# Row maximum of a streamed tensor: other load sizes, and a last row without halves

## The chip, the cores and the metric

The kernel runs on one core of a Trainium2 chip. The metric is the device time of one execution in microseconds (us). Executions of the kernel before took 166.0 to 166.5 us.

Names used below: DVE is VectorE, which does the reductions. SP is SyncE, whose queue issues the loads. ACT is ScalarE, whose queue issues the two stores. A load is cut into packets, one for each of 128 partitions, and 16 DMA engines move 8 of these packets each. A load has *landed* when its semaphore has been stepped by all 16 of them.

## The reference

```python
batch, seq, dim = 32, 512, 1024
x = np.random.randn(batch, seq, dim).astype(np.float32)   # 67.1 MB

def reference(x):
    return np.max(x, axis=-1).astype(np.float32)          # 16384 maxima
```

The 16,384 rows are dealt out to 128 partitions, 128 rows each. Below, "a row" is one row on every partition at once: 128 x 1024 elements, 512 KB.

## The kernel before

It streams the input into a ring of 46 rows in SBUF. Each load brings some rows to all partitions, and one reduction on DVE follows each load. Load sizes fall towards the end, so that little is left to reduce when the last byte has come. The last row is loaded and reduced in two halves, and a maximum combines them.

```python
ROWS = [10, 13, 12, 10, 9, 8, 7, 7, 6, 5, 5, 4, 4, 3, 3, 3, 3, 2, 2, 2, 2, 2, 1, 1, 1, 1, 1]
RING = 46
...
    for g in ROWS:
        if at + g > RING:
            at = 0
        xc = ring[:, at:at + g, :]
        nc.sync.dma_start(out=xc, in_=xr[:, b:b + g, :])
        nc.vector.reduce_max(out=res[:, b:b + g], in_=xc, axis=X)
        at += g
        b += g
        if not stored and b >= I - 16:      # I = 128: the results of 112 rows go out early
            stored = b
            nc.scalar.dma_start(out=out_r[:, :b], in_=res[:, :b])

    assert b == I - 1 and at + 1 <= RING
    for h in range(2):                      # the last row, in halves
        xh = ring[:, at, h * H:(h + 1) * H]
        nc.sync.dma_start(out=xh, in_=xr[:, b, h * H:(h + 1) * H])
        nc.vector.reduce_max(out=part[:, h:h + 1], in_=xh, axis=X)
    nc.vector.tensor_tensor(out=res[:, b:b + 1], in0=part[:, 0:1], in1=part[:, 1:2],
                            op=mybir.AluOpType.max)
    nc.scalar.dma_start(out=out_r[:, stored:], in_=res[:, stored:])
```

A load into a part of the ring that still holds unreduced rows waits until they are reduced. The trace shows a second limit: the loads and stores share eight semaphores, so a ninth DMA waits for the first to land.

Of the kernel before, what the change touches and what calls it, by code (L numbers as in the profile page):

```python
# [1 line left out]

# [4 lines left out]


F32 = mybir.dt.float32


ROWS = [10, 13, 12, 10, 9, 8, 7, 7, 6, 5, 5, 4, 4, 3, 3, 3, 3, 2, 2, 2, 2, 2, 1, 1, 1, 1, 1]
RING = 46


@with_exitstack
def kernel(
    ctx: ExitStack,
    tc: tile.TileContext,
    x: bass.AP,  # L20
    out: bass.AP,
):
    nc = tc.nc
    P = 128
    X = mybir.AxisListType.X

    xf = x.flatten_outer_dims()
    N, D = xf.shape
    H = D // 2
    I = N // P  # L30

    xr = xf.rearrange("(p i) d -> p i d", p=P)
    of = out.flatten_outer_dims()
    out_r = bass.AP(tensor=of.tensor, offset=of.offset, ap=[[I, P], [1, I]])

    once = ctx.enter_context(tc.tile_pool(name="once", bufs=1))
    ring = once.tile([P, RING, D], F32)
    res = once.tile([P, I], F32)
    part = once.tile([P, 2], F32)

    b = at = 0
    stored = 0
# [8 lines that stand above are left out]
        if not stored and b >= I - 16:  # L51
            stored = b
            nc.scalar.dma_start(out=out_r[:, :b], in_=res[:, :b])

    assert b == I - 1 and at + 1 <= RING
    for h in range(2):
        xh = ring[:, at, h * H:(h + 1) * H]
        nc.sync.dma_start(out=xh, in_=xr[:, b, h * H:(h + 1) * H])
        nc.vector.reduce_max(out=part[:, h:h + 1], in_=xh, axis=X)  # L59
    nc.vector.tensor_tensor(  # L60
        out=res[:, b:b + 1], in0=part[:, 0:1], in1=part[:, 1:2],
        op=mybir.AluOpType.max,
    )
    nc.scalar.dma_start(out=out_r[:, stored:], in_=res[:, stored:])


# [1 line left out]
_INS = ['x']  # L68
_OUTS = [((32, 512), 'float32')]


# [23 lines left out]
```

## Time and profile before

| what | value | where it is read |
|---|---|---|
| time, median of four runs | 166.22 us | the runs |
| span of the profiled run | 164.7 us | the page |
| first load (10 rows) lands | 15.80 us | semaphore records |
| last load (half a row) lands | 160.74 us | semaphore records |
| DVE's last instruction ends | 162.40 us | timeline |
| the last store lands | 163.85 us | semaphore records |

The page of the kernel before: the span and DVE's busy time (busy, share of the span, instructions); the span in 40 slices, with busy tenths of DVE and of the DMA engines; the chain of waits by line; and the groups of DVE's instructions (busy us, mean ns of one | idle before them, and what ended it).

```profile
span 164.7 us, 118 instructions
DVE 139.5 (85%) x30; POOL 0.2 (0%) x4
...
DVE  0001994399989999999999989999999999999994
...
DMA  6998999999989999999999999999999999999960
...
DMA ring<-in_x_dram 70%; DVE res L48 27%; DVE part L59 1%; DVE res L60 0%
...
L48 DVE TENSOR_REDUCE res<-ring 128x2 f32<-128x2048 f32 (+11 forms) x27 | 138.1, 5165 | 22.9 <-DMA ring<-in_x_dram 22.7
L59 DVE TENSOR_REDUCE part<-ring 128x1 f32<-128x512 f32 x2 | 1.3, 676 | 0.0
L60 DVE TENSOR_TENSOR res<-part 128x1 f32<-128x1 f32 x1 | 0.2, 159 | 0.0
```

The slices decide: the DMA engines are busy from the second slice to the 38th, whereas DVE idles for much of the first eight and catches up. DVE's 85% is large only because the two rates are close. The groups kept apart by shape give DVE's rate:

```profile
L48 DVE TENSOR_REDUCE res<-ring 128x10 f32<-128x10240 f32 x2 | 21.6, 10816 | 15.8 <-DMA ring<-in_x_dram 15.8
...
L48 DVE TENSOR_REDUCE res<-ring 128x13 f32<-128x13312 f32 x1 | 14.0, 14020 | 4.9 <-DMA ring<-in_x_dram 4.9
...
L48 DVE TENSOR_REDUCE res<-ring 128x1 f32<-128x1024 f32 x5 | 5.7, 1208 | 0.0
```

Three more rows cost 14.020 - 10.816 = 3.204 us, that is 1.068 us a row, plus 0.14 us an instruction. Five single rows are busy for only 5.7 us with overlaps counted once, not 6.0: the next one starts 0.08 us before the one in front has ended, so one starts every 1.13 us. The loads bring a row every 1.23 us on average, a single row every 1.28 us.

Last, the timeline of the end of the kernel before (start us, us, engine, line, operation, count; "q" marks the issue of a DMA):

```profile
158.69 2.33 DVE L48 TENSOR_REDUCE res<-ring 128x1 f32<-128x1024 f32 x2
160.94 1.27 DVE L59 TENSOR_REDUCE part<-ring 128x1 f32<-128x512 f32 x2
162.25 0.16 DVE L60 TENSOR_TENSOR res<-part 128x1 f32<-128x1 f32 x1
162.44 0.34 ACTq L64 DMA_DIRECT2D out_dram<-res  x1
```

The last half has landed at 160.74 us, when DVE has not yet begun even the first half. 1.66 us pass from that landing to the end of the maximum.

### The profile page before, as it was taken

Reading aid. Unit: us, or ns where it says so; the run is one execution under the profiler, and the core shown is the slowest. Engines: PE = TensorE matmul, PEld = TensorE weight load, DVE = VectorE, ACT = ScalarE, POOL = GpSimd, SP = SyncE. Lnnn points to the kernel's source line nnn. Section 1 sums busy time; section 2 is a strip of 40 time slices with the busy share of each in tenths; the row PEclk is TensorE's granted clock in tenths of the full one; section 3 lists DMA queues with packets and bytes.
Section 4 is the critical chain, followed back from the end, with each engine's and each line's share of the span. In section 5 each row is a group of like instructions: output and inputs, shape, how many; then the busy total and the mean of one; then the engine's idle time right before and its main releaser. Section 6 shows DMA issues by size and latency. Waiting matters only on the chain.

```text
span 164.7 us, 118 instructions
## 1 busy us (share of the span) xinstructions
DVE 139.5 (85%) x30; POOL 0.2 (0%) x4
## 2 busy tenths in 40 slices
DVE  0001994399989999999999989999999999999994
POOL 0000000000000000000000000000000000000000
DMA  6998999999989999999999999999999999999960
GB/s 199 438 467 376 453 465 453 436 406 394 469 388 467 444 430 430 408 438 425 439 432 425 426 431 419 428 438 409 438 430 421 427 421 421 420 418 421 408 260 2
DMA packets 4464, 67.18 MB, mean 408 GB/s; under 512 B 752, under 2 KB 752, under 8 KB 1648
## 3 DMA queue, kind: packets, MB, share of 16 engines
q1 hardware_dynamic: 4176, 67.11, 95.8%
q10 hardware_dynamic: 288, 0.07, 0.2%
HBM read 67.11 MB, written 0.07 MB: 408 GB/s over the span
## 4 chain that ended last, share of the span: by engine, by line
DMA 70%; DVE 28%; issue 0%
DMA ring<-in_x_dram 70%; DVE res L48 27%; DVE part L59 1%; DVE res L60 0%
## 5 line engine op out<-in xcount | busy, mean ns | idle before, releaser
L48 DVE TENSOR_REDUCE res<-ring 128x2 f32<-128x2048 f32 (+11 forms) x27 | 138.1, 5165 | 22.9 <-DMA ring<-in_x_dram 22.7
L59 DVE TENSOR_REDUCE part<-ring 128x1 f32<-128x512 f32 x2 | 1.3, 676 | 0.0
L60 DVE TENSOR_TENSOR res<-part 128x1 f32<-128x1 f32 x1 | 0.2, 159 | 0.0
L79 POOL MEMSET const-bfloat16-1.0<- 128x1 bf16 x1 | 0.1, 101 | 0.0
L79 POOL MEMSET const-uint8-127<- 128x1 uint8 x1 | 0.1, 101 | 0.0
L79 POOL MEMSET const-float32-0.0<- 128x1 f32 x1 | 0.1, 98 | 0.2 <-issue 0.2
L79 POOL MEMSET const-float32-1.0<- 128x1 f32 x1 | 0.1, 98 | 0.0
## 6 DMA issues: line engine op xcount, KB each, us to landing
ring<-in_x_dram SPq DMA_DIRECT2D x2, 5120.0 KB, 35.6
ring<-in_x_dram SPq DMA_DIRECT2D x2, 3584.0 KB, 33.0
ring<-in_x_dram SPq DMA_DIRECT2D x1, 6656.0 KB, 30.4
ring<-in_x_dram SPq DMA_DIRECT2D x1, 6144.0 KB, 44.4
ring<-in_x_dram SPq DMA_DIRECT2D x4, 1536.0 KB, 38.9
ring<-in_x_dram SPq DMA_DIRECT2D x2, 2560.0 KB, 38.1
ring<-in_x_dram SPq DMA_DIRECT2D x5, 1024.0 KB, 22.2
ring<-in_x_dram SPq DMA_DIRECT2D x1, 4608.0 KB, 43.1
```

The costliest lines, as they stand in the source:

```text
L48: nc.vector.reduce_max(out=res[:, b:b + g], in_=xc, axis=X)
L59: nc.vector.reduce_max(out=part[:, h:h + 1], in_=xh, axis=X)
L60: nc.vector.tensor_tensor(out=res[:, b:b + 1], in0=part[:, 0:1], in1=part[:, 1:2], op=mybir.AluOpType.max,)
L79: nc = _bacc.Bacc("TRN2", target_bir_lowering=False, num_devices=1)
```

## The change

The intent: the sizes start at 14 and fall without a rise, there are eight single rows at the end in place of five, and the last row comes whole, so that there is no second reduction and no combining maximum behind it.

```diff
-ROWS = [10, 13, 12, 10, 9, 8, 7, 7, 6, 5, 5, 4, 4, 3, 3, 3, 3, 2, 2, 2, 2, 2, 1, 1, 1, 1, 1]
+ROWS = [14, 14, 11, 11, 9, 8, 8, 7, 6, 5, 5, 4, 4, 3, 3, 2, 2, 2, 2, 1, 1, 1, 1, 1, 1, 1, 1]
...
-    assert b == I - 1 and at + 1 <= RING
-    for h in range(2):
-        xh = ring[:, at, h * H:(h + 1) * H]
-        nc.sync.dma_start(out=xh, in_=xr[:, b, h * H:(h + 1) * H])
-        nc.vector.reduce_max(out=part[:, h:h + 1], in_=xh, axis=X)
-    nc.vector.tensor_tensor(
-        out=res[:, b:b + 1], in0=part[:, 0:1], in1=part[:, 1:2],
-        op=mybir.AluOpType.max,
-    )
+    assert b == I
     nc.scalar.dma_start(out=out_r[:, stored:], in_=res[:, stored:])
```

Both lists reach row 112 at the end of a load: the old one after 17 loads, the new one after 15. The first 112 rows are the *head*, the last 16 the *tail*.

More of the change, by code (lines that the diff above doesn't have):

```diff
@@ L28 @@
     N, D = xf.shape
-    H = D // 2
     I = N // P
@@ L38 @@
     res = once.tile([P, I], F32)
-    part = once.tile([P, 2], F32)
     b = at = 0
```

## The prediction

> **What bounds the kernel now.** The stream of loads. The page's busy line says VectorE (DVE) 85%, but its slices show the DMA engines near 0.9 from the second slice to the 38th. From the landing of the first load (10 rows, 15.80 us) to that of the last two-row load (122 rows in all, 153.08 us) a row takes 1.226 us, 428 GB/s; by the groups by form, reductions take 1.068 us a row plus 0.14 us an instruction (13 rows 14.02 us, one row 1.21 us). DVE is faster than the loads and runs behind only by what one load brings at once. The Trainium skill, "VectorE: DVE Perf Modes", perf-mode tier table, gives tensor_reduce only the 1x mode; 1024 elements at its 0.96 GHz are 1.067 us, as this trace has it. "DMA: Bandwidth & Descriptors", Specifications, gives a fabric ceiling of 435 GB/s; at 428, no load pattern can gain much there. The chain of waits credits DVE with 28%, but most of that is backlog absorbed by the next landing.
>
> **What counts** is: the start, 128 rows of stream, and what follows the last landing. Before: the last half row lands at 160.74, DVE still has 0.8 us of backlog and starts it at 161.54, ends 162.21; the maximum ends at 162.40; the store is issued at 162.44, lands at 163.85; end 164.7.
>
> **What the change does.**
> - First load 14 rows: DVE starts near 20.6 instead of 15.8 us. Off the critical path: it catches up at 0.137 us a row.
> - Only three loads (39 of 46 rows) fit before the ring wraps, where four did. The fourth waits for the first reduction (ends about 35.7 us), but the queue holds work until about 50. I stepped through the ring, the limit of eight DMAs in flight and both rates: the smallest margin in mid-run is about 9 us. The first store still leaves at row 112, near 144 us, and lands near 150.6; a single-row load that reuses its semaphore waits for it, with about 1.8 us of queued work left. Tight, but enough.
> - DMA overhead: about 0.075 us a load (one row 1.28 us, three rows 3.69 us). 27 loads for 29; but the halves landed 0.62 to 0.63 us apart, so the gain is 0.05 to 0.15 us.
> - Tail: eight singles land every 1.28 us and DVE takes 1.12 us from start to start, so the backlog of about 0.8 us shrinks by 0.16 each and is gone before the last. The last reduction starts as its row lands and takes 1.21 us. Before, landing to end of the maximum was 1.66 us. Gain 0.45 us, less any residue.
>
> **Sum.** -0.1 (loads) -0.4 (tail) = -0.5 us of 166.26: 165.8 us; range 165.2 to 166.5. Faster by over 2%: 1%; within 2%: 98%; slower: 1%.
>
> **What would show it.** The last load lands at 160.5 to 160.8; one reduction of 1.21 us stands behind it and no maximum; DVE idles 20.6 us at first; DMA slices stay at 9; no gap of the load stream near 152 us.
>
> **What would make it wrong.** (1) One DMA engine fell 0.67 us behind the other fifteen at 65.9 us (a 36,864-byte packet took 2.15 us instead of 1.36) and every later load ended on it. If that is chance, the difference can be anything between 0 and -1.1 us. (2) The single-row load that waits for the store leaves the queue empty: up to 1 us lost. (3) Backlog left at the last row: up to 0.5 us lost.

(The 1.067 us a row that it works out from the page's clock is an estimate; the trace's own figure is the 1.068 us.)

## The result, and the profile after

The changed kernel took 165.62 us (median of four runs, 165.41 to 165.81) against 166.22 us (166.00 to 166.53). The ratio is 0.9962, with a 95% interval of 0.9942 to 0.9982. Here and below a ratio is the mean time of one kernel's fast runs over that of the other's fast runs of the same rounds, so it is not quite the ratio of the medians that are quoted. The forecast was 165.8 us and "within 2%".

The same lines of the page after:

```profile
span 163.8 us, 111 instructions
DVE 138.7 (85%) x27; POOL 0.2 (0%) x4
...
DVE  0000099978999999999999999999999999999993
...
DMA  6999999989999989999999999999999999999980
...
DVE res L46 57%; DMA ring<-in_x_dram 41%; SPq L45 0%
...
L46 DVE TENSOR_REDUCE res<-ring 128x1 f32<-128x1024 f32 (+10 forms) x27 | 138.7, 5202 | 22.7 <-DMA ring<-in_x_dram 22.6
```

DVE starts at 20.75 us in place of 15.82 and idles 22.7 us in all, against 22.9 us before: the late start is made up while the DMA slices stay full. A trap in this page is the chain of waits. DVE's share doubles, from 28% to 57%, though DVE does less work and the loads still set the pace. The last piece of that chain, in order of time, is:

```profile
94.69 66.64 DVE res L46 x21
```

After the reduction that starts at 94.69 us DVE has no gap: each one starts just before the one in front has ended, 0.02 to 1.01 us after its own row landed, so the chain never steps over to a load. Only the last of these lags counts.

The end of the changed kernel, from the timeline:

```profile
157.81 3.52 DVE L46 TENSOR_REDUCE res<-ring 128x1 f32<-128x1024 f32 x3
161.37 0.34 ACTq L54 DMA_DIRECT2D out_dram<-res  x1
```

The table sets the landings of the last pieces, from the semaphore records, beside the starts of their reductions, from the instruction records. The lag is the difference.

| before: piece | lands | starts | lag | after: piece | lands | starts | lag |
|---|---|---|---|---|---|---|---|
| | | | | single 1 | 151.18 | 152.18 | 1.00 |
| single 1 | 154.36 | 155.31 | 0.95 | single 3 | 153.74 | 154.43 | 0.69 |
| single 3 | 156.92 | 157.56 | 0.64 | single 5 | 156.30 | 156.68 | 0.38 |
| single 5 | 159.49 | 159.82 | 0.33 | single 7 | 158.86 | 158.94 | 0.08 |
| first half | 160.12 | 160.94 | 0.82 | single 8 | 160.09 | 160.11 | 0.02 |
| second half | 160.74 | 161.54 | 0.80 | | | | |

The single rows wear the backlog down by 0.155 us each, in both kernels. Before, the halves build it up again: the first half lands 0.63 us after a single row that takes DVE 1.2 us.

Between the two profiled runs the difference is 164.73 - 163.82 = 0.91 us. That is more than the 0.60 us between the medians: the profiled run of before, at 166.5 us, stands at the slow end of its four. It splits into three parts:

| part | before | after | difference |
|---|---|---|---|
| start to the last landing | 160.74 | 160.09 | -0.65 |
| last landing to DVE's last end | 1.66 | 1.24 | -0.42 |
| DVE's last end to the end of the span | 2.33 | 2.49 | +0.16 |

The second line is the tail that was predicted. The other two raised questions.

**The first line.** The prediction had seen that one DMA engine fell 0.67 us behind in the profile of before. The steps of the last load's semaphore put a number on it: fifteen engines were done at 160.10 us before and at 160.07 us after, and the sixteenth at 160.74 and at 160.09. So by the undisturbed engines the stream was shorter by only 0.03 us. But was the delay chance, or did the old sizes invite it?

**The third line** turned out to be SP's closing sequence. After its last load SP waits for the eight DMA semaphores in pairs, in a fixed order, with four instructions about 0.07 us apart. Here are SP's waits for the output in the view of waits (us in total, times, longest), first before, then after:

```profile
SPq L90 <- DMA out_dram<-res: 3.1, 1, 3.1
```

```profile
SPq L80 <- DMA out_dram<-res: 11.4, 1, 11.4
```

With 29 loads and two stores, the last store used a semaphore of the third pair; the first two pairs had been passed before it landed. With 27 loads it uses one of the first pair: SP stops there for 11.4 us, and has three more waits to walk through afterwards. From the landing of the store to the end of the span it is 0.88 us before and 1.01 us after; the rest of the 0.16 us is the store itself, 1.42 us from issue to landing before and 1.45 after.

### The profile page after: what moved, and what is told of

It reads as the page before. It is cut to its first block, busy times and chain, and to the rows that moved or that the text cites. A ratio compares the mean times of both kernels' runs of the same rounds, so it can differ in the third digit from the quotient of the medians.

```text
span 163.8 us, 111 instructions
## 1 busy us (share of the span) xinstructions
DVE 138.7 (85%) x27; POOL 0.2 (0%) x4
## 4 chain that ended last, share of the span: by engine, by line
DVE 57%; DMA 41%; SPq 0%; issue 0%
DVE res L46 57%; DMA ring<-in_x_dram 41%; SPq L45 0%
## 5 line engine op out<-in xcount | busy, mean ns | idle before, releaser
L46 DVE TENSOR_REDUCE res<-ring 128x1 f32<-128x1024 f32 (+10 forms) x27 | 138.7, 5202 | 22.7 <-DMA ring<-in_x_dram 22.6
```

## The experiments

Theory A: what lasts of the gain is behind the last landing; the heads differ only by two loads, and the rest of the first line is one engine's chance delay. Rival B: the new sizes make the stream itself shorter, or spare it such delays.

Twelve runs were made, in three calls of four, each call on one chip, which are named P, Q and R in order. Chip and time of a call are not parted by this: "chip Q" below means the chip at the time of that call. (The chip of the first comparison is not known.) All results were correct. The kernel before ran beside each call: 166.94 us on P (166.1 to 167.81), 167.00 on Q (166.35 to 167.32), 165.93 on R (165.87 to 166.26). No two calls can be compared by raw times.

### New head alone (chip P)

The kernel before, old tail with halves and maximum, with the head of the changed one:

```diff
-ROWS = [10, 13, 12, 10, 9, 8, 7, 7, 6, 5, 5, 4, 4, 3, 3, 3, 3, 2, 2, 2, 2, 2, 1, 1, 1, 1, 1]
+ROWS = [14, 14, 11, 11, 9, 8, 8, 7, 6, 5, 5, 4, 4, 3, 3, 2, 2, 2, 2, 2, 1, 1, 1, 1, 1]
```

> Only the load sizes of the first 112 rows are the new ones; the last 16 rows, the halves and the maximum are as before. Theory A (all of the lasting gain is in what follows the last landing, and the 0.65 us by which the last load landed earlier in the profile is one DMA engine's chance delay): the time is that of before within 0.15 us (ratio 0.999 to 1.001), landing of the last load to end of the maximum stays 1.66 us. Rival B (the new sizes of the large loads make the stream shorter, or keep an engine from falling behind): 0.3 to 0.65 us faster (ratio 0.996 to 0.998), last load landing near 160.1.

Measured: 166.16 us (165.85 to 166.50, six runs), ratio 0.9958 (0.9930 to 0.9986). From last landing (160.51) to the end of the maximum it is 1.66 us again:

```profile
160.71 1.27 DVE L59 TENSOR_REDUCE part<-ring 128x1 f32<-128x512 f32 x2
162.01 0.16 DVE L60 TENSOR_TENSOR res<-part 128x1 f32<-128x1 f32 x1
```

The tail behaves as theory A says, but the time does not. Theory A expected no gain and the interval excludes that: on this chip the new head was worth something by itself. This went for rival B, though not in every point: B had the last load land near 160.1 us, and in this profile, which has late DMA packets (below), it landed at 160.51.

### New tail alone (chip P)

```diff
-ROWS = [10, 13, 12, 10, 9, 8, 7, 7, 6, 5, 5, 4, 4, 3, 3, 3, 3, 2, 2, 2, 2, 2, 1, 1, 1, 1, 1]
+ROWS = [10, 13, 12, 10, 9, 8, 7, 7, 6, 5, 5, 4, 4, 3, 3, 3, 3, 2, 2, 2, 2, 1, 1, 1, 1, 1, 1, 1, 1]
(and no halves, no maximum, as in the changed kernel)
```

> Only the last 16 rows are the new ones (four loads of two rows, eight of one, no halves, no maximum); the first 112 rows are as before. Theory A: 0.4 us faster than before (ratio 0.997 to 0.998), last landing to end of the last reduction 1.21 to 1.25 us. Rival B: within 0.15 us of before, because the stream is what got shorter.

Measured: 166.43 us (165.44 to 166.95), ratio 0.9968 (0.9934 to 1.0002). The last row lands at 160.10 us and its reduction, below, ends 1.24 us later.

```profile
160.13 1.22 DVE L46 TENSOR_REDUCE res<-ring 128x1 f32<-128x1024 f32 x1
```

The profile is what theory A expected (1.21 to 1.25 us). The ratio agrees with it too but is not clear of 1; the clean measure came later, on chip R.

### Before, with a whole last row (chip P)

```diff
-ROWS = [10, 13, ..., 2, 1, 1, 1, 1, 1]
+ROWS = [10, 13, ..., 2, 1, 1, 1, 1, 1, 1]
(and no halves, no maximum, as in the changed kernel)
```

It parts the tail's gain into the halves' going and the longer row of singles.

> Before, with its last row loaded and reduced whole: no halves and no maximum, six single rows at the end where the changed kernel has eight. Theory A: DVE still starts the last row about 0.17 us after it landed (the backlog shrinks by 0.155 us a single), so last landing to end is about 1.38 us and the gain 0.25 us (ratio 0.998 to 0.999): more than half of the tail's gain is the halves' going, the rest the longer row of singles. If the halves' going were all, it would be 0.42; if it were nothing, 0. Rival B: no gain.

Measured: 166.73 us (166.01 to 167.37), ratio 0.9982 (0.9946 to 1.0019): not clear of 1. The profile is clearer. The last row lands at 161.15 us, and the reduction starts 0.27 us later and ends 1.48 us after the landing:

```profile
161.42 1.21 DVE L46 TENSOR_REDUCE res<-ring 128x1 f32<-128x1024 f32 x1
```

The expectation was a lag of 0.17 us. The last two rows had landed only 1.24 and 1.22 us apart, not 1.28, so the backlog shrank less. Of the 0.42 us, the halves' going is 1.66 - 1.48 = 0.18 us in this profile, and the two further singles 0.24 us: the reverse of the shares that I had expected. But this profile is one of those with late DMA packets (below). With landings 1.28 us apart the lag would have been about 0.95 - 5 x 0.155 = 0.17 us, an estimate from the lags above, and the shares 0.28 and 0.14 us, so the split is not settled.

### The changed kernel, with halves at the end (chip P)

```diff
-ROWS = [14, 14, 11, 11, 9, 8, 8, 7, 6, 5, 5, 4, 4, 3, 3, 2, 2, 2, 2, 1, 1, 1, 1, 1, 1, 1, 1]
+ROWS = [14, 14, 11, 11, 9, 8, 8, 7, 6, 5, 5, 4, 4, 3, 3, 2, 2, 2, 2, 1, 1, 1, 1, 1, 1, 1]
(and the last row in two halves with the maximum, as before)
```

> The changed kernel with its last row in two halves and the maximum put back, all other sizes the new ones. Theory A: the first half lands 0.65 us after the seventh single row, whose reduction takes 1.2 us, so DVE meets both halves with a backlog of about 0.5 us; last landing to end about 1.35 us, end 0.15 to 0.2 us later than the changed kernel's, still 0.25 us faster than before. A rival that I held when I planned it: after enough singles the backlog is gone, so halves would end 0.9 us after the last landing, 0.3 us earlier than the changed kernel.

Measured: 165.82 us (165.51 to 166.26), ratio 0.9938 (0.9909 to 0.9967). The timeline:

```profile
158.74 1.22 DVE L48 TENSOR_REDUCE res<-ring 128x1 f32<-128x1024 f32 x1
159.86 1.27 DVE L59 TENSOR_REDUCE part<-ring 128x1 f32<-128x512 f32 x2
161.17 0.16 DVE L60 TENSOR_TENSOR res<-part 128x1 f32<-128x1 f32 x1
```

The halves land at 159.32 and 159.94 us; DVE begins the first 0.54 us late and ends 1.39 us after the last landing. Counted from the landing of the seventh single row, DVE ends after 161.33 - 158.66 = 2.67 us here and after 161.33 - 158.86 = 2.47 us in the changed kernel. So halves cost 0.20 us even where no backlog stands before them. The rival about the halves (0.3 us to be won) is out: a first half lands too soon after a whole row. The time gives no verdict on this, since this kernel ran in no call beside the changed one. Beside the kernel before it was 1.0 us faster, where 0.25 had been expected: again the new head brought more than theory A allows.

On chip P the two kernels with the new head had medians of 165.82 and 166.16 us, the two with the old head and a changed tail 166.43 and 166.73 us. The packet records of the six profiles so far tell where the difference may come from. A packet is called late here when it took over 0.3 us longer than the median of its size; those of the first load at the start, which all are slow, are left out.

```
profile               late packets, the worst   in which load, when (us)
before                2, 0.78 us                9 rows (36,864 B), 65.7 to 65.9
after                 0
new head alone        8, 0.96 us                11 rows (45,056 B), 43.0 to 43.8
new tail alone        4, 0.37 us                12 rows (49,152 B), 33.9 to 34.4
whole last row        11, 1.40 us               9 rows, 62.3 to 63.1
halves at the end     0
```

What a late packet costs can be read from the time between the first and the last of the 16 steps of a landing, 0.8 to 1.0 us in the loads before it. In the profile of before it rose to 1.56 us at the 9-row load, in that of the new head alone to 1.50 at the 11-row load, in that of the whole last row to 2.06 at the 9-row load; it was still 1.50, 1.27 and 2.02 us at the last load, so most of the delay was never made up. In the profile of the new tail alone it stayed at 0.96 us, so there the late engines must have been ahead of the others. All late packets are over 32 KB. This became theory C: when engines are delayed, the old head loses more to it.

### The changed kernel again, and the old head again (chip Q)

> The changed kernel once more, as the mark for the three runs beside it. The runs before this one left a difference that theory A did not foresee: kernels with the new first 112 rows were 0.75 us faster than those with the old ones, where A has 0.15 us (two loads fewer at 0.075 us). Theory C: in a spell in which DMA engines stall often, the old sizes lose more to stalls; then this is 0.9 to 1.2 us faster than before (ratio 0.993 to 0.9955). Theory A with chance alone: 0.55 us faster (ratio 0.9965), as 0.4 for the tail and 0.15 for two loads fewer.

> The old first 112 rows with the new last 16, once more. Theory C: 0.5 to 0.8 us slower than the changed kernel beside it. Theory A: 0.15 us slower.

"Old head again" is the same kernel as "new tail alone". Measured: the changed kernel 165.55 us (165.34 to 166.23), ratio 0.9927 (0.9904 to 0.9949); the old head 166.43 us (165.77 to 166.64), ratio 0.9957 (0.9935 to 0.9979). Their tails are the same, 1.24 us in both profiles. The difference is the head alone: 0.88 us between the medians, 0.58 us between the means of six runs each. The ranges overlap (the old head's fastest run took 165.77 us), so its size is rough. Theory A had 0.15 us; theory C had 0.5 to 0.8 us. Against the kernel before, C had 0.993 to 0.9955 for the changed kernel and A 0.9965: A's value lies outside the interval, and the measured 0.9927 just beyond C's range on the faster side. The profile of the changed kernel has no late packet; that of the old head has 4 in the 12-row load at 41.2 to 41.5 us and 10 in the 9-row load at 62.3 to 63.3 us.

### Four loads that fit the ring, sizes falling (chip Q)

```diff
-ROWS = [14, 14, 11, 11, 9, 8, 8, 7, 6, 5, 5, 4, 4, 3, 3, 2, ...]
+ROWS = [12, 12, 11, 11, 9, 8, 8, 7, 6, 5, 5, 4, 4, 4, 3, 3, 2, ...]
```

> New last 16 rows; the first four loads are 12, 12, 11 and 11 rows, which just fill the ring of 46, so that four loads are queued at once as in the old head, but sizes fall without a rise as in the new one. If it is the number of loads queued at the start that lets stalls cost more, this is as slow as old_head_again; if it is the rise in size after a 10-row first load, it is as fast as after_again, within 0.2 us. Theory A: between the two, within 0.15 us of both.

Measured: 166.56 us (165.39 to 167.35), ratio 0.9967 (0.9932 to 1.0003). Eight packets of the 9-row load, at 66.4 to 67.0 us, were 1.3 to 1.6 us late. It was as slow as the old head beside it, which by the expectation speaks for the number of loads queued at the start. A falling order does not protect, nor does a first load over 10 rows. Its single runs lay anywhere between 165.39, as fast as the changed kernel, and 167.35 us.

### A head of small loads (chip Q)

```diff
-ROWS = [14, 14, 11, 11, 9, 8, 8, 7, 6, 5, 5, 4, 4, 3, 3, 2, ...]
+ROWS = [8, 8, 8, 7, 7, 7, 7, 7, 8, 8, 7, 6, 5, 5, 4, 4, 3, 3, 2, ...]
```

> New last 16 rows; the first 59 rows in loads of 8 and 7 in place of 14, 14, 11, 11 and 9, so no packet is over 32 KB. In the six profiles so far every packet that took over 0.3 us too long was one of 36 KB or more, in the first 67 us. If long packets are what stalls, the profile has no such packet, and the time is that of after_again plus 0.23 us for three more loads, with less scatter. If the stalls belong to the time and not to the size, they come here too, in packets of 28 or 32 KB, and the time scatters as in the others.

Measured: 165.63 us (165.33 to 165.99), ratio 0.9920 (0.9900 to 0.9939), no late packet in the profile. Six loads (45 of 46 rows) were queued at the start here, so a full ring at the start does not by itself invite delays, at least with packets of 32 KB or less. The three further loads cost less than the 0.23 us expected: 0.08 us between the medians. Part of that is the closing sequence, for the last store had the fourth pair and the end came 0.81 us after its landing in place of 1.01.

### Four attempts at the cause (chip R)

What remained: the late packets sit mostly in the 9-row load in fifth place, behind four large loads. Is it its size, its source rows, its place in the ring, or the time at which it is issued? Each of four kernels changes one of these.

```diff
(old head, new tail)              -RING = 46
                                  +RING = 44
(the changed kernel)              -RING = 46
                                  +RING = 50
(old head, new tail)              -ROWS = [10, 13, 12, 10, 9, 8, 7, 7, 6, 5, 5, 4, ...]
                                  +ROWS = [10, 13, 12, 10, 10, 8, 7, 7, 5, 5, 5, 4, ...]
(old head, new tail)              -in_=xr[:, b:b + g, :]
                                  +in_=xr[:, I - b - g:I - b, :]    (results and stores alike)
```

> Old first 112 rows and new last 16, with the ring cut from 46 to 44 rows, and nothing else: sizes, source rows and order of loads stay, but the fourth load no longer fits at once and waits for the first reduction, as in the changed kernel; the 9-row load is written to rows 10 to 19 of the ring and issued near 45.6 us in place of 26.6. Theory D (the delays come from what is queued at the start and when the loads behind it are issued, or from where in the ring they go): no packet over 0.3 us late, median within 0.3 us of 165.6. Theory E (they come from the sizes or the source rows of the old head): median 166.2 to 166.6 and late packets in the 9-row load between 60 and 68 us, as in old_head_again.

> The changed kernel with a ring of 50 rows in place of 46, nothing else: now its first four loads (14, 14, 11, 11) fill the ring at once, the 9-row load goes to rows 0 to 9 and is issued near 35.8 us in place of 52.8. Theory D: it gets the delays of the old head, median 166.0 or more, late packets near 66 us. Theory E: as the changed kernel, median 165.4 to 165.7, no packet over 0.3 us late after 60 us.

> Old head and new tail, with the fifth load of 10 rows in place of 9 (and the ninth of 5 in place of 6). In five profiles with four loads queued at the start, the late packets of over 1 us, and most of the others, were the 36,864-byte ones of the 9-row load in fifth place. If that size is the cause, they are gone and the median is 165.7 or less; if the place or the time is, the 40,960-byte packets in the same place are late at 60 to 68 us and the median is 166.2 or more.

> Old head and new tail, with the rows of each partition read from the last to the first: same sizes, same ring, same times of issue, other source addresses (the fifth load reads rows 74 to 82 in place of 45 to 53). If the source addresses are the cause, the delays go or move and the median falls to 165.7 or less; if the schedule is, they stay between 60 and 68 us and the median stays 166.2 or more.

Measured:

| kernel | median us (range), five runs | ratio to before (95%) | late packets |
|---|---|---|---|
| old head, ring of 44 | 165.47 (165.41 to 165.57) | 0.9972 (0.9958 to 0.9985) | 0 |
| changed kernel, ring of 50 | 165.49 (165.43 to 165.95) | 0.9975 (0.9963 to 0.9988) | 0 |
| old head, 10 rows for 9 | 165.54 (165.51 to 165.88) | 0.9977 (0.9964 to 0.9989) | 0 |
| old head, rows reversed | 165.52 (165.46 to 165.71) | 0.9974 (0.9961 to 0.9986) | 0 |

As a test of theories D and E the call failed: on chip R the kernel before itself ran undisturbed, at 165.93 us with a spread of 0.4, and nothing was delayed that could have been cured. Three different changes "cured" the old head here, which is the sign that there was nothing to cure. What the late packets depend on stays open.

The call is good for something else. It is the only one in which the tail is measured without that disturbance. All four kernels have the new tail, three have an old head, each with one more change: 0.38 to 0.46 us faster than before (0.23% to 0.28% of 165.93), where the tail's profile says 0.42. And the new head (ring of 50) gains nothing over old ones: 165.49 against 165.47 to 165.54. Its last row lands at 160.02 us, theirs at 160.06, 160.19 and 160.12, which is 0.04 to 0.17 us earlier for two loads fewer; the closing sequence takes 0.13 us back (1.01 for 0.88 us).

That closing cost follows the semaphore of the last store in all fourteen profiles: 1.01 us from landing to end where the store is in the first pair (27 loads, four profiles), 0.94 in the second (28 loads, three), 0.88 in the third (29 loads, six) and 0.81 in the fourth (30 loads, one).

The profiled runs of all calls, put side by side, show the same disturbance. Eight of the fourteen have no late packet, and they took 165.34 to 165.60 us whatever their head and chip. Of the six with late packets one took 165.44 us (the new tail alone, where the delay was made up), and the other five 165.81 to 166.81 us (two of these have the old tail, which is worth 0.42). This suggests that what parts the heads on P and Q is how often and how hard a run is delayed, not how long an undisturbed run takes.

## Why the prediction was right or wrong

It was right on the time: 165.8 us forecast, 165.62 measured. That alone tests little, for the range of 165.2 to 166.5 us also held the 166.22 us of the kernel before, and part of the hit is luck: one term was left out (the closing sequence), and a gain that was not forecast came in (fewer delays). The steps say more, and they fared unequally.

- *The stream of loads bounds the kernel, DVE only trails it.* Right. DVE began 4.9 us later and nothing was lost; "DVE starts near 20.6" was 20.75 us.
- *The fourth load waits for the first reduction, at no cost.* Right: issued at 35.86 us (35.7 forecast), and the DMA slices stay full.
- *The load that waits for the early store is tight but not late.* Right. The store landed at 150.12 us, the load was issued at 150.14 and landed 1.28 us after the one in front, as all its neighbours.
- *The tail gains 0.45 us less any residue.* Right: 0.42 us in the profiles (1.66 to 1.24), 0.38 to 0.46 us in the times on chip R, where three old heads carry the new tail. The lag at the last row was 0.02 us.
- *Two loads fewer gain 0.05 to 0.15 us.* Single profiles on chip R show 0.04 to 0.17 us and the undisturbed engines of the first pair 0.03 us, so the size fits but is not well measured. The sum lacked a term: with 27 loads the last store falls on the first pair of SP's closing waits and 0.13 us is given back. I had not looked at what stands behind the store.
- *The last load lands at 160.5 to 160.8 us.* Wrong: 160.09. The text had named the reason as its first doubt, the engine that fell behind at 65.9 us in the profile of before.
- *If that is chance.* This is what the runs do not leave standing as it was put. The delays do differ from run to run, and with the call, by its chip or its time: before runs at 165.93 us on R and at 167.0 us on Q. But where they come they do not hit all kernels alike. On Q the old head lost 0.6 us by the means (0.9 by the medians) against the new one with the same tail, and on P the new head alone was 0.7 us faster than before (ratio 0.9958). So the change has a second gain, between nothing (R, with a ring of 50) and some 0.6 us (Q), that I did not predict.

By the terms, undisturbed, the change is worth, as an estimate, -0.42 (tail) - 0.10 (loads) + 0.13 (closing) = -0.39 us. The first comparison gave -0.60 us. The remaining 0.2 us fits a few delayed runs of before, which had values up to 166.53 there against 165.87 to 166.26 on R, but this was not tested by itself.

Why the old head, and the head of 12, 12, 11 and 11, suffer more than one of 14, 14, 11 and 11 or one of sevens and eights is not known. It is not the rise in size, nor by itself the number of rows queued at the start. Four loads of long packets queued at once remain a candidate: both heads that suffered had that (45 and 46 rows), the changed kernel has three (39 rows), and the ring of 44 and the ring of 50, which were to test it, met no delays. That long packets are needed is suggested, not shown: no profile had a late packet of 32 KB or less, but only one kernel had such packets alone, and only one of its six runs was profiled. They are not enough: the changed kernel has long packets and mostly escapes (of the four profiles of its head with a ring of 46, one has late packets).

## What to carry to other kernels

At the end of a stream, do not ask how small the last piece is but when the engine behind it can begin: pieces must shrink no faster than the engine works off the one in front, or the last piece meets a backlog and its small size buys nothing. Follow the path past the last result, too: here the number of DMAs decides which closing wait the last store meets, worth up to 0.2 us. And before reading a difference of half a microsecond between two profiles as an effect of the sizes, look at the sixteen steps of the last landing: if one engine alone is late, repeat the pair beside each other, on more than one chip and at more than one time.

## What the Trainium skill lacked or had wrong

- "DMA: Bandwidth & Descriptors", Anatomy of one DMA, gives a fixed cost of about 2.0 us for one transfer, and its section Bandwidth advises at least 1 MiB for 75% of the peak, from transfers on another path (issued from GpSimd). For loads queued behind each other from SP the page has a rate at 1 MiB a load, among measurements of another path, but none for smaller loads and no cost of one load more. The runs show both: loads of one row (512 KB) land every 1.28 us, 410 GB/s, and a load more costs only about 0.075 us. The 435 GB/s that the page gives as the fabric's ceiling agrees with 428 GB/s over most of the stream here.
- "VectorE: DVE Perf Modes", the TRN2 errata, has 58 cycles plus one for each element, and says that this is too short for one instruction. Both hold here: a reduction of 1024 elements takes 1.208 us, but one starts every 1.13 us. An estimate by the page's formula, (58 + 1024) / 0.96 GHz, is 1.127 us. The page does not say that its row is the interval from start to start ("Vector Engine (DVE) Microarchitecture Reference" has a fixed cost for queued instructions, but does not link it to this row).
- No page tells that DMA engines can be delayed for a while, in some calls and not in others: up to 14 packets of one run 0.3 to 1.6 us late, all of 36 KB or more and before 70 us, on two chips where the kernel before had medians of 166.9 and 167.0 us. On a third, where four profiles had no such packet, it had 165.93 us. Whether the chip or the time decides was not tested.
- No page tells of the closing sequence at the end of such a kernel: 0.07 us for each further pair of DMA semaphores that stands behind the last store's, 0.81 to 1.01 us from its landing to the end.
